# Split weight products: the low part of the weights last in each projection, and new priorities for the streams of the mixers

## The chip, the cores and the metric

The kernel runs on one core of one Trainium2 chip. The metric is the device time of one execution in microseconds (us), the median of several executions. A core has five engines with a queue each: TensorE (PE, with its weight loads shown apart as PEld), VectorE (DVE), ScalarE (ACT), GpSimd (POOL) and SyncE (SP). They wait for one another through semaphores. Matmul results land in eight banks of PSUM, and a bank is used again only when the engine that reads it out has finished.

## The reference

Two decoder layers on 256 tokens of width 1024, then a final RMSNorm. One combined projection feeds three groups of heads: gated delta net (GDN, six heads), native sparse attention (NSA, six query heads) and stick breaking (SB, four heads).

```python
for i in range(DEPTH):                      # DEPTH = 2
    hn = rmsnorm(h, ln_mix[i])
    (g_q, g_k, g_v, g_z, g_a, g_b, n_q, n_kc, n_vc, n_ks, n_vs, n_kw, n_vw, n_gate,
     s_q, s_k, s_v) = jnp.split(hn @ w_in[i], SPLIT_POINTS, axis=-1)
    o_gdn = gated_deltanet(...)
    o_nsa = native_sparse_attention(...)
    o_sb = stick_breaking_attention(s_q, s_k, s_v)
    mix = jnp.concatenate([o_gdn, head_rmsnorm(o_nsa, nsa_norm[i]), head_rmsnorm(o_sb, sb_norm[i])], axis=-1)
    h = h + mix @ w_out[i]
    h = h + conv_ffn(rmsnorm(h, ln_ffn[i]), w_up[i], ffn_conv[i], w_down[i])
    gate = jax.nn.sigmoid(rmsnorm(h, ln_ple[i]) @ w_ple_gate[i])
    h = h + gate * rmsnorm(p[i] @ w_ple[i], ple_norm[i])
return rmsnorm(h, ln_final)
```

## The kernel before

**Three products for one.** Each large matrix product is made of three. A weight piece `wr_*` comes by DMA (SP queue), ACT copies it into a rounded high part `wh_*`, and DVE subtracts the two into the low part `wl_*`, in halves of 512 columns. The activations `XH` and `XL` are split likewise. Then PE adds high times high, high times low and low times high in one bank. A piece is used for eight steps k over the width of 1024.

**The stages of a layer.** The mixers come first. PE runs their projections in the order g1, k, kcvc, g2, g3, v, q, sq, sk, sv. The pieces of k, v and q (three each) end in a causal convolution `cv` or `cq`: ACT scales the bank, and DVE adds three shifted copies, which frees the bank. Beside the projections the heads' own work runs. For NSA that is `Va`, the transposes of the rotated queries and keys to `qT` and `KH`, the split into `QQ` and `KL`, the scores (`b<-KH,QQ`, `b<-KL,QQ` and a mask), a maximum `mx` on DVE, an exponential `P` on ACT, a transpose by PE (`b<-cst,P`), a copy `PT` on ACT, and the product with `Va`. For GDN it is an inverse by a chain of some thirty small DVE operations that alternate between `prod` and `Tb`, then a copy `Tq` and matrix products with `Ta`, `Ab`, `Z` and `H`. For SB it is `L`, `b<-L,cst` and what follows. After the mixers come the output projection, the FFN (22 steps of gate `ga`, up `up` and down `dn`), and a gate.

**What sets the order.** All of it is laid out when the program is built, and each engine then runs its list as it stands. The pieces of work are generators that say what they need (`need`). `drive` looks at a model of the engines' clocks, takes those streams whose needs are met within `early` microseconds of PE's model clock, and steps the one with the lowest priority number. The projections are priority 5; `PLAN` has the numbers of the others, one dictionary for each layer. `inverse` is the chain of `Tb`, `gdn`, `nsa` and `sb` are the groups of heads, `cmp`, `compress`, `heads` and `finish` parts of NSA, `out` and `tokens` parts of GDN. `slack` and `fslack` say how far ahead of PE's model clock a weight piece may be split, in the mixers and in the rest.

`pieceA` adds one piece of k, v, q, sq, sk, and of the FFN's `ga` and `up`; `piecesB` adds those of g2, g3 and sv. `pieceA` waits per step for the low part, too:

```python
for k in range(0, KT, self.plan["step"]):
    yield self.need(0, W[1], X[1])
    self.projA(out, X, W, range(k, k + self.plan["step"]))
```

Every operation is issued through one helper, so the profile shows line L352 for nearly all; the names tell them apart.

Of the kernel before, what the change touches and what calls it, by code (L numbers as in the profile page):

```python
# [18 lines left out]
T = 256  # L19
D = 1024  # L20
KT = D // 128
HD = 64
# [400 lines left out]
class Trunk:  # L423
# [3 lines left out]
    PLAN = (dict(pace=1.0, early=0.2, slack=5, fslack=6, step=1, gdn=0, nsa=0, sb=0, inverse=2,  # L427
                 tokens=3, out=0, compress=-1, cmp=2, heads=1, finish=1, pair=4),
            dict(pace=1.1, early=0.3, slack=3, fslack=8, step=1, gdn=1, nsa=0, sb=2, inverse=2,
                 tokens=3, out=2, compress=0, cmp=4, heads=3, finish=0, pair=2))  # L430
# [221 lines left out]

    def added(self):
        return self.splitting[4] if self.splitting else self.n_split < len(self.split_seq) and self.by_transfer()

    def by_transfer(self):
        l, n, i = self.split_seq[self.n_split][:3]
        return n in self.ADDED and not self.spare(n, i) and self.n_split >= self.n_take + 2
# [277 lines left out]
    def pieceA(self, name, i, out, X, fresh=False):  # L936

        W = self.take(name, i)
        if fresh:
            mm = self.t.matmul  # L940
# [8 lines left out]
        for k in range(0, KT, self.plan["step"]):  # L949
            yield self.need(0, W[1], X[1])  # L950
            self.projA(out, X, W, range(k, k + self.plan["step"]))
        self.done()

    def piecesB(self, name, n, outs, cols, X, nk):
        for i in range(n):
            W = self.take(name, i)
            for t in range(2):
                for k in range(nk):
                    yield self.need(0, W[1], self.of(t))
                    self.projB(outs[t][:, :cols], X, W, t, i * nk, [k])  # L960
            self.done()
# [228 lines left out]
    def gdn(self, l):  # L1190
        v, a, g, gp, c, m = self.v, self.a, self.g, self.gp, self.c, self.m
        mm = self.t.matmul
# [57 lines left out]
        for r, lhs, msk, dst in ((r1, "incl", "m_strict", dec), (r2, "gt", "m_incl", decT)):  # L1250
            for x in range(2):
# [3 lines left out]
                   start=False, stop=True)  # L1255
# [24 lines left out]
        def blocks():  # L1280


            n = 24 * (64 // NB)
# [7 lines left out]
            D = self.dram.tile([2, 6, 128, 64], F32, name=f"D{l}")  # L1291
            for x in range(2):
                v.tensor_mul(fl(A[x]), bs[x][:, 0:384], fl(dec[x]))
# [13 lines left out]
            yield self.need(0, M, Tb)  # L1307
            for j in range(NB - 1):
                if j and j % 3 == 0:
                    yield self.pause(1)  # L1310
# [21 lines left out]
            yield self.need(0, F)  # L1332
            return A16, F
# [184 lines left out]
        for ch in range(4):  # L1518
            t, cp = divmod(ch, 2)
# [595 lines left out]
```

## Time and profile before

| | |
|---|---|
| median of 3 runs | 837.64 us (837.6 to 843.46) |
| the profiled execution, its own time | 837.27 us |
| its span | 835.5 us |
| mean granted TensorE clock | 0.984 |
| PE busy | 811.6 us (97%) |
| DVE busy | 626.3 us (75%) |
| ACT busy | 478.8 us (57%) |
| POOL busy | 77.4 us (9%) |
| HBM read, written | 128.29 MB, 2.03 MB |
| chain that ended last | PE 80%, DVE 10%, ACT 4%, DMA 2%, issue 2%, POOL 1% |

Busy time of matmuls is modelled at its end, so the distance from one start to the next says more than a matmul's own duration. The granted clock is 1.00 at 2.4 GHz and 0.50 at 1.2 GHz; a stretch's number is the mean over it. The first layer's mixers fill about the span's first 180 us, the second's begin near 419 us.

### The profile page before, as it was taken

How to read it: one execution, taken by the hardware profiler on the slowest of the kernel's cores; microseconds unless marked ns; L12 is line 12 of the kernel's file. 1: busy time of each engine (PE TensorE's matmuls, PEld its weight loads, DVE VectorE, ACT ScalarE, POOL GpSimd, SP SyncE). 2: the span in 40 equal slices, each digit the busy share in tenths (PEclk: the TensorE clock that was granted, in tenths of full speed). 3: DMA queues.
4: the chain of work that ended last, by engine and by line, in shares of the span. 5: the costliest groups of instructions: out<-in, count | busy, mean ns of one | idle time of the engine just before them, and what ended most of it. 6: DMA issues, size and time to landing. Idle time of an engine off the chain costs nothing.

```text
span 835.5 us, 16816 instructions
## 1 busy us (share of the span) xinstructions
PE 811.6 (97%) x6529; PEld 736.3 (88%) x6529; DVE 626.3 (75%) x1337; ACT 478.8 (57%) x1043; POOL 77.4 (9%) x151
## 2 busy tenths in 40 slices
PE   8999899999999999999999979999999999999996
PEld 6989778888999999998998868888899999999986
DVE  5748988677887788876775688967588878788755
ACT  6546474556665566554655465627476556566543
POOL 2012000211100000000301100021110000000012
PEclk9999899999999999999999997999999999999999
DMA  8645230235676677753565414203446556676501
GB/s 310 251 163 150 66 110 28 77 123 154 201 227 186 188 214 220 218 189 96 152 233 186 134 69 111 86 27 102 151 152 227 202 181 202 220 209 219 176 30 51
DMA packets 50591, 131.40 MB, mean 157 GB/s; under 512 B 17104, under 2 KB 18000, under 8 KB 50512
## 3 DMA queue, kind: packets, MB, share of 16 engines
q1 hardware_dynamic: 49056, 125.42, 47.4%
q0 software_dynamic: 1312, 4.72, 1.7%
q8 instruction: 51, 0.84, 0.4%
q14 instruction: 28, 0.23, 0.1%
q10 hardware_dynamic: 144, 0.20, 0.1%
HBM read 128.29 MB, written 2.03 MB: 156 GB/s over the span
## 4 chain that ended last, share of the span: by engine, by line
PE 80%; DVE 10%; ACT 4%; DMA 2%; issue 2%; POOL 1%; SPq 0%; POOLq 0%; DVEq 0%; ACTq 0%
PE b L352 80%; DVE wl_g L352 1%; DMA wr_w1v<-in_w_dram 1%; DVE Tb L352 1%; DVE cv L352 1%; DVE prod L352 1%; DVE oq L352 1%; ACT XH L352 1%; DMA wr_g<-in_w_dram 1%; DVE XL L352 0%; DVE QQ L352 0%; DMA wr_q<-in_w_dram 0%; ACT xh L352 0%; ACT wh_g L352 0%; DVE wl_k L352 0%
## 5 line engine op out<-in xcount | busy, mean ns | idle before, releaser
L352 DVE SCALAR_TENSOR_TENSOR u<-b,pc,u 128x255 f32<-128x255 f32 (+1 forms) x176 | 84.7, 481 | 41.1 <-ACT u L352 37.9
L352 PE MATMUL b<-XL,wh_up 128*128 128x256 f32 x352 | 99.7, 283 | 0.0
L352 PE MATMUL b<-XH,wl_up 128*128 128x256 f32 x352 | 99.6, 283 | 0.0
L352 PE MATMUL b<-XH,wh_up 128*128 128x256 f32 x352 | 99.6, 283 | 0.0
L352 PE MATMUL b<-XH,wl_ga 128*128 128x256 f32 x352 | 99.0, 283 | 0.0
L352 PE MATMUL b<-XH,wh_ga 128*128 128x256 f32 x352 | 99.0, 283 | 0.0
L352 PE MATMUL b<-XL,wh_ga 128*128 128x256 f32 x352 | 97.3, 283 | 0.0
L352 ACT ACTIVATE u<-b,pc 128x256 f32<-128x256 f32 x88 | 41.5, 472 | 74.8 <-PE b L352 74.8
L352 PE MATMUL b<-wl_dn,ah 128*128 128x512 f32 x176 | 69.3, 394 | 0.0
L352 PE MATMUL b<-wh_dn,al 128*128 128x512 f32 x176 | 69.2, 393 | 0.0
L352 PE MATMUL b<-wh_dn,ah 128*128 128x512 f32 x176 | 69.2, 393 | 0.0
L352 PEld LDWEIGHTS b<-XH,wh_ga 128*128 128x128 f32 x352 | 66.9, 190 | 1.7
L352 PEld LDWEIGHTS b<-XL,wh_ga 128*128 128x128 f32 x352 | 66.0, 190 | 1.5
L352 PEld LDWEIGHTS b<-XL,wh_up 128*128 128x128 f32 x352 | 67.1, 191 | 0.0
L352 PEld LDWEIGHTS b<-XH,wh_up 128*128 128x128 f32 x352 | 67.1, 191 | 0.0
L352 PEld LDWEIGHTS b<-XH,wl_up 128*128 128x128 f32 x352 | 67.1, 191 | 0.0
L352 PEld LDWEIGHTS b<-XH,wl_ga 128*128 128x128 f32 x352 | 67.0, 190 | 0.1
L352 DVE TENSOR_TENSOR wl_ga<-wr_ga,wh_ga 128x512 fp32r<-128x512 f32 x88 | 56.9, 688 | 6.1 <-ACT wh_ga L352 2.6
L352 DVE TENSOR_TENSOR wl_up<-wr_up,wh_up 128x512 fp32r<-128x512 f32 x88 | 56.6, 685 | 0.4
L352 DVE TENSOR_TENSOR wl_dn<-wr_dn,wh_dn 128x512 fp32r<-128x512 f32 x88 | 56.5, 684 | 0.4
L352 ACT ACTIVATE ah<-sg 128x256 fp32r<-128x256 f32 x44 | 18.4, 418 | 64.8 <-DVE sg L352 64.8
L352 ACT ACTIVATE wh_up<-wr_up 128x512 fp32r<-128x512 f32 x88 | 50.2, 620 | 0.0
(385 smaller groups left out, 2209.7 us busy)
## 6 DMA issues: line engine op xcount, KB each, us to landing
wr_ga<-in_w_dram SPq DMA_DIRECT2D x44, 512.0 KB, 3.8
wr_up<-in_w_dram SPq DMA_DIRECT2D x44, 512.0 KB, 4.2
wr_dn<-in_w_dram SPq DMA_DIRECT2D x44, 512.0 KB, 3.6
wr_out<-in_w_dram SPq DMA_DIRECT2D x16, 512.0 KB, 3.5
wr_pg<-in_w_dram SPq DMA_DIRECT2D x16, 512.0 KB, 3.3
row<-in_rows_dram POOLq DMA_DIRECT2D x8, 512.0 KB, 4.1
wr_g<-in_w_dram SPq DMA_DIRECT2D x8, 512.0 KB, 5.5
wr_g<-in_w_dram SPq DMA_DIRECT2D x8, 414.0 KB, 3.3
```

What stands on the lines that cost most here:

```text
L352: return f(*args, **kw)
```

## The change

Two things are changed. In `pieceA` and `piecesB` all products with the high part of a piece come first and wait for the high part alone; those with the low part come last and wait for it then. `pieceA` is used by the FFN as well, so the FFN's order changes too. And `PLAN` has other numbers: in the first layer seven (`early`, `slack`, `gdn`, `sb`, `inverse`, `out`, `cmp`), in the second six (`fslack`, `gdn`, `nsa`, `inverse`, `compress`, `cmp`). A flag `quiet` is added that never becomes true (`j >= 99` in a loop of fifteen) and guards a branch that the empty `ADDED` already closes. Kinds and counts of matmuls, of the operations on DVE, ACT and POOL and of the DMAs stay the same.

```diff
-    PLAN = (dict(pace=1.0, early=0.2, slack=5, fslack=6, step=1, gdn=0, nsa=0, sb=0, inverse=2,
-                 tokens=3, out=0, compress=-1, cmp=2, heads=1, finish=1, pair=4),
-            dict(pace=1.1, early=0.3, slack=3, fslack=8, step=1, gdn=1, nsa=0, sb=2, inverse=2,
-                 tokens=3, out=2, compress=0, cmp=4, heads=3, finish=0, pair=2))
+    PLAN = (dict(pace=1.0, early=0.3, slack=2, fslack=6, step=1, gdn=3, nsa=0, sb=4, inverse=4,
+                 tokens=3, out=4, compress=-1, cmp=4, heads=1, finish=1, pair=4),
+            dict(pace=1.1, early=0.3, slack=3, fslack=6, step=1, gdn=-1, nsa=3, sb=2, inverse=-2,
+                 tokens=3, out=2, compress=3, cmp=0, heads=3, finish=0, pair=2))
...
-        for k in range(0, KT, self.plan["step"]):
-            yield self.need(0, W[1], X[1])
-            self.projA(out, X, W, range(k, k + self.plan["step"]))
+        mm = self.t.matmul
+        for k in range(KT):
+            yield self.need(0, W[0], X[1])
+            for x in X:
+                mm(out, W[0][:, k], x[:, k], start=k == 0 and x is X[0], stop=False)
+        for k in range(KT):
+            yield self.need(0, W[1])
+            mm(out, W[1][:, k], X[0][:, k], start=False, stop=k == KT - 1)
         self.done()
...
-            for t in range(2):
-                for k in range(nk):
-                    yield self.need(0, W[1], self.of(t))
-                    self.projB(outs[t][:, :cols], X, W, t, i * nk, [k])
+            for q, xs in ((0, X), (1, X[:1])):
+                for t in range(2):
+                    s = slice(t * 128, t * 128 + 128)
+                    for k in range(nk):
+                        yield self.need(0, W[q], self.of(t))
+                        self.M.part = t
+                        for x in xs:
+                            mm(outs[t][:, :cols], x[:, i * nk + k, s], W[q][:, k], start=(q, i, k) == (0, 0, 0) and x is X[0],
+                               stop=(q, i, k) == (1, n - 1, nk - 1))
+                        self.M.part = None
```

The first place is DVE in the mixers of the second layer, where the chain of `Tb` and `prod` ends. Before, the row of the maxima `mx` of the first two heads stands directly behind the chain:

```order
L352 TENSOR_TENSOR prod<-Mb,Tb 96x15
L352 TENSOR_TENSOR Tb<-Tb,prod 96x15
L352 CAST Tq<-Tb 96x256 x2
L352 TENSOR_REDUCE mx<-b 128x2 x4
L352 SCALAR_TENSOR_TENSOR cv<-b,pc_193,cv 128x255
L352 SCALAR_TENSOR_TENSOR cv<-b,pc_193,cv 128x254
L352 SCALAR_TENSOR_TENSOR cv<-b,pc_193,cv 128x253
L352 TENSOR_TENSOR wl_q<-wr_q,wh_q 128x512 x2
```

And now the same end of the chain:

```order
L352 TENSOR_TENSOR prod<-Mb,Tb 96x15
L352 TENSOR_TENSOR Tb<-Tb,prod 96x15
L352 CAST Tq<-Tb 96x256 x2
L352 SCALAR_TENSOR_TENSOR cv<-b,pc_193,cv 128x255
L352 SCALAR_TENSOR_TENSOR cv<-b,pc_193,cv 128x254
L352 SCALAR_TENSOR_TENSOR cv<-b,pc_193,cv 128x253
L352 TENSOR_TENSOR KL<-b,KH_6095 64x512
L352 TENSOR_TENSOR QQ_6093<-qT,QQ_6093 64x768
L352 TENSOR_TENSOR KL<-b,KH_6096 64x512
L352 TENSOR_TENSOR QQ_6094<-qT,QQ_6094 64x768
```

The chain moved ahead of the splits `KL` and `QQ`: 17 of its operations stand ahead of the last two rotations of the keys (`kr` and `ropet`), and 12 behind them. The maxima come two `cv` and four `wl_q` rows after `QQ`, clear of the chain.

The second place is ACT there, from `Va` on. Before, the copy of the first q piece stands behind `Va`:

```order
L352 ACTIVATE Va<-b 128x4x64 x2
L352 ACTIVATE wh_q<-wr_q 128x512 x2
L352 ACTIVATE qT<-b 128x3x128 x2
L352 ACTIVATE KH_6030<-b 64x512
L352 ACTIVATE KH_6031<-b 64x512
L352 ACTIVATE KH_6030<-KH_6030 64x512
L352 ACTIVATE QQ_6028<-qT 64x768
L352 ACTIVATE KH_6031<-KH_6031 64x512
L352 ACTIVATE QQ_6029<-qT 64x768
L352 ACTIVATE cv<-b,pc_193 128x256 x3
```

And now:

```order
L352 ACTIVATE Va<-b 128x4x64 x2
L352 ACTIVATE cv<-b,pc_193 128x256
L352 ACTIVATE qT<-b 128x3x128 x2
L352 ACTIVATE KH_6095<-b 64x512
L352 ACTIVATE KH_6096<-b 64x512
L352 ACTIVATE KH_6095<-KH_6095 64x512
L352 ACTIVATE QQ_6093<-qT 64x768
L352 ACTIVATE KH_6096<-KH_6096 64x512
L352 ACTIVATE QQ_6094<-qT 64x768
L352 ACTIVATE cv<-b,pc_193 128x256
L352 ACTIVATE wh_q<-wr_q 128x512 x2
```

The copy `wh_q` of the first q piece moved behind the whole preparation of `KH` and `QQ` and behind two `cv`. On PE the first twelve products of that piece now stand ahead of the first scores; before, the scores of the first two head pairs stood among the products of v, ahead of all of q.

The third place is DVE in the first layer, where the chain begins. Before, the splits stand ahead of the chain, and two `cv` as well:

```order
L352 TENSOR_TENSOR QQ_975<-qT,QQ_975 64x768
L352 SCALAR_TENSOR_TENSOR cv<-b,pc_189,cv 128x255
L352 SCALAR_TENSOR_TENSOR cv<-b,pc_189,cv 128x254
L352 SCALAR_TENSOR_TENSOR cv<-b,pc_189,cv 128x253
L352 TENSOR_TENSOR wl_q<-wr_q,wh_q 128x512 x2
L352 SCALAR_TENSOR_TENSOR cv<-b,pc_189,cv 128x255
L352 SCALAR_TENSOR_TENSOR cv<-b,pc_189,cv 128x254
L352 SCALAR_TENSOR_TENSOR cv<-b,pc_189,cv 128x253
L352 TENSOR_TENSOR Tb<-Tb,Mb 96x15
L352 TENSOR_TENSOR prod<-Mb,Tb 96x28
```

And now, from the fifth operation of the chain on:

```order
L352 TENSOR_TENSOR Tb<-Tb,prod 96x13x3
L352 TENSOR_TENSOR KL<-b,KH_981 64x512
L352 TENSOR_TENSOR QQ_979<-qT,QQ_979 64x768
L352 TENSOR_TENSOR KL<-b,KH_982 64x512
L352 TENSOR_TENSOR QQ_980<-qT,QQ_980 64x768
L352 TENSOR_TENSOR prod<-Mb,Tb 96x48
L352 TENSOR_TENSOR Tb<-Tb,prod 96x12x4
```

Five operations of the chain moved ahead of the splits, twelve more stand between `QQ` and the first `cv` of v, and the last twelve and `Tq` between the first `cv` and the second; the `mx` of the first heads come behind the second `cv`.

## Rows read from the trace of the kernel before

**Rows 1.** The page: busy time, share and count of each engine.
```profile
PE 811.6 (97%) x6529; PEld 736.3 (88%) x6529; DVE 626.3 (75%) x1337; ACT 478.8 (57%) x1043; POOL 77.4 (9%) x151
```

**Rows 2.** Busy time by stretches of 20 us, with the granted clock (PEclk).
```profile
core 0: us, PE busy (x) PEld busy (x) DVE busy (x) ACT busy (x) POOL busy (x), PEclk, DMA share, GB/s
...
80.00:100.00 20.00, 16.77 (x124) 14.39 (x122) 18.52 (x63) 10.45 (x27) 0.45 (x1) 0.95 0.16 47
100.00:120.00 20.00, 18.95 (x166) 15.82 (x165) 18.30 (x47) 13.92 (x28) 2.44 (x5) 0.88 0.49 136
...
220.00:240.00 20.00, 20.00 (x142) 18.74 (x141) 17.92 (x35) 13.02 (x29) 0.92 (x2) 1.00 0.72 217
...
480.00:500.00 20.00, 14.95 (x118) 13.88 (x116) 15.97 (x50) 11.92 (x28) 0.66 (x2) 0.94 0.21 79
500.00:520.00 20.00, 19.95 (x154) 16.57 (x153) 17.00 (x44) 9.60 (x24) 1.38 (x3) 0.72 0.42 112
...
560.00:580.00 20.00, 18.83 (x158) 16.66 (x159) 13.91 (x34) 13.45 (x28) 6.31 (x7) 1.00 0.29 94
```

**Rows 3.** Timeline of PE in the first layer's FFN: start, duration, operation, idle before.
```profile
250.07 0.28 PE L352 MATMUL b<-XH,wh_ga 128*128 128x256 f32 x1
...
250.90 0.28 PE L352 MATMUL b<-XL,wh_ga 128*128 128x256 f32 x1
```

**Rows 4.** Groups of PE's instructions: busy, mean ns, idle before and releasers.
```profile
L352 PE MATMUL b<-cst,P 128*128 128x128 f32 x72 | 11.8, 304 | 5.5 <-DVE mx L352 4.6 <-ACT P L352 0.9
...
L352 PE MATMUL b<-KH,QQ 128*128 128x256 f32 (+1 forms) x24 | 8.7, 427 | 3.8 <-DVE cq L352 1.7 <-DVE on L352 1.0 <-DVE QQ L352 0.9
L352 PE MATMUL b<-L,cst 128*128 128x384 f32 (+1 forms) x32 | 7.9, 388 | 0.9 <-DVE L L352 0.9
```

**Rows 5.** Timeline of PE in the second layer, scores, q, and transposes of P.
```profile
486.98 0.28 PE L352 MATMUL b<-KH,QQ 128*128 128x256 f32 x1
...
491.19 0.28 PE L352 MATMUL b<-XH,wh_q 128*128 128x256 f32 x1
...
493.95 0.28 PE L352 MATMUL b<-XH,wl_q 128*128 128x256 f32 x1
498.84 1.54 PE L352 MATMUL b<-cst,P 128*128 128x128 f32 x6 [4.61 <-DVE mx L352]
```

**Rows 6.** Timeline of DVE there: last rotation, chain's first, maxima.
```profile
479.76 0.35 DVE L352 TENSOR_TENSOR ropet<-b,sin 128x64 f32<-128x64 f32 x2
...
489.01 0.18 DVE L352 TENSOR_TENSOR Tb<-Tb,Mb 96x15 f32<-96x15 f32 x1
...
497.72 1.41 DVE L352 TENSOR_REDUCE mx<-b 128x2 f32<-128x256 f32 x4
```

**Rows 7.** Timeline of ACT there, from Va to the convolutions.
```profile
479.75 0.85 ACT L352 ACTIVATE Va<-b 128x256 f32<-128x256 f32 x2 [1.36 <-DVE ropet L352]
480.49 1.14 ACT L352 ACTIVATE wh_q<-wr_q 128x512 fp32r<-128x512 f32 x2
481.53 0.86 ACT L352 ACTIVATE qT<-b 128x384 f32<-128x384 f32 x2
...
486.39 0.84 ACT L352 ACTIVATE cv<-b,pc 128x256 f32<-128x256 f32 x2
```

**Rows 8.** Timeline of DVE in the first layer: split, chain, convolutions.
```profile
80.08 0.95 DVE L352 TENSOR_TENSOR QQ<-qT,QQ 64x768 fp32r<-64x768 f32 x1
...
88.05 0.20 DVE L352 TENSOR_TENSOR prod<-Mb,Tb 96x48 f32<-96x48 f32 x1
...
90.94 1.50 DVE L352 SCALAR_TENSOR_TENSOR cv<-b,pc,cv 128x255 f32<-128x255 f32 x3
...
95.14 0.58 DVE L352 CAST Tq<-Tb 96x256 f16<-96x256 f32 x2
95.63 1.51 DVE L352 SCALAR_TENSOR_TENSOR cq<-b,pc,cq 128x255 f32<-128x255 f32 x3
```

**Rows 9.** Timeline of PE in the first layer, the first product of q.
```profile
84.68 0.28 PE L352 MATMUL b<-XH,wh_q 128*128 128x256 f32 x1
```

More of the change, by code (lines that the diff above doesn't have):

```diff
@@ L651 @@
     ADDED = ()
+    quiet = False
     def added(self):
@@ L657, in by_transfer @@
         l, n, i = self.split_seq[self.n_split][:3]
-        return n in self.ADDED and not self.spare(n, i) and self.n_split >= self.n_take + 2
+        return n in self.ADDED and not self.spare(n, i) and not self.quiet and self.n_split >= self.n_take + 2
     def split_to(self, n):
@@ L948, in pieceA @@
             return
-        for k in range(0, KT, self.plan["step"]):
-            yield self.need(0, W[1], X[1])
-            self.projA(out, X, W, range(k, k + self.plan["step"]))
+        mm = self.t.matmul
[6 more added lines that the diff above has]
+            mm(out, W[1][:, k], X[0][:, k], start=False, stop=k == KT - 1)
         self.done()
     def piecesB(self, name, n, outs, cols, X, nk):
+        mm = self.t.matmul
         for i in range(n):
             W = self.take(name, i)
-            for t in range(2):
-                for k in range(nk):
-                    yield self.need(0, W[1], self.of(t))
-                    self.projB(outs[t][:, :cols], X, W, t, i * nk, [k])
+            for q, xs in ((0, X), (1, X[:1])):
[8 more added lines that the diff above has]
+                        self.M.part = None
             self.done()
@@ L1291, in blocks @@
             D = self.dram.tile([2, 6, 128, 64], F32, name=f"D{l}")
+            self.quiet = False
             for x in range(2):
@@ L1307, in blocks @@
             yield self.need(0, M, Tb)
+            self.quiet = False
             for j in range(NB - 1):
+                self.quiet = j >= 99
                 if j and j % 3 == 0:
@@ L1332, in blocks @@
             yield self.need(0, F)
+            self.quiet = False
             return A16, F
```

## Prediction

> **What bounds the kernel now.** I read the busy time of the engines first. PE is busy for 97% of the span, and the next engine for 75% [rows 1]. So only time in which PE stands, or runs at its lower clock, can be won; the change removes no matmul. Next the stretches of 20 us show where such time lies. In the FFN PE is busy for 20.00 of 20 us at a granted clock of 1.00 (220 to 240 us) [rows 2]. The mixers have three bad places: 80 to 120 us in the first layer (16.77 and 18.95 us busy, clock 0.95 and 0.88), 480 to 520 us in the second (14.95 us busy and then a clock of 0.72), and 560 to 580 us (18.83 us busy) [rows 2]. The groups of PE's instructions then name what PE waited for: DVE's `mx` for 4.6 us ahead of the transposes of `P`, and DVE's `cq`, `on` and `QQ` for 1.7, 1.0 and 0.9 us ahead of scores [rows 4]. The timelines of PE, DVE and ACT give the order of events. So in the mixers DVE, busy with the chain of `Tb`, is what ends last.
>
> **What the low clock costs.** The clock has two levels, 2.4 and 1.2 GHz, so a mean of 0.88 is a low level in 24% of the stretch. In the first layer the low time is 20 x (0.10 + 0.24) = 6.8 us, in the second 20 x (0.12 + 0.56) = 13.6 us, from the clocks of [rows 2]. Work done then takes twice as long, so at most 3.4 and 6.8 us are lost. The part of the low time in which PE stands anyway costs nothing: if all of the low time before 100 us and before 500 us (2.0 and 2.4 us) lay in waits, the loss would be 2.4 and 5.6 us. I take 3.1 and 6.1, together 9.2 us, with 8.0 and 10.2 as the ends. The clock fell after the 4.6 us wait for `mx`, and in the first layer after waits of 1.7 and 1.0 us close together [rows 2, 4]. The Trainium skill, "TensorE: Matmul & The Clock Gate", section Terms, puts the penalty at the throttled time times the withheld share of the clock, which would be 10.2 us for these stretches and an end about 1 us lower than mine. That page counts low time in waits as well; the trace here has such time, so I stay with 9.2.
>
> **The products' order by itself: nothing in the FFN.** Matmuls with 256 columns start 0.12 us apart whichever product follows which (eight starts from 250.07 to 250.90, seven steps of 0.119 us) [rows 3]. High products first and low products last are the same 24 starts, and where PE never waits (20.00 of 20 us) a later need for the low part saves nothing. What hides a late low part there is PE's own backlog; if it were gone, a whole DVE subtraction would show. I cost the FFN at 0, with 0 to 1 us as the bound, since a stretch without idle time could only lose. In the mixers the order matters only with the new priorities.
>
> **First layer, 80 to 110 us.** Before, PE waited 1.7 (`cq`), 1.0 (`on`), half of 0.9 (`QQ`, shared by both layers) and 0.9 us (ACT `P`): 4.05 us [rows 4]. Now twelve operations of the chain stand between the last `QQ` and the first `cv` of v. The split `QQ` ends at 81.03; twelve such operations took 90.94 - 88.05 = 2.9 us, and three rows of `cv` 1.5 us, so the bank of the first `cv` is free at 81.03 + 2.9 + 1.5 = 85.4 [rows 8]. That is the bank that q's first piece takes, and PE comes to it at 84.68 [rows 9]: a wait of 0.7 us. The next twelve operations are the shorter ones (95.14 - 90.94 - 1.5 = 2.7 us), `Tq` takes 0.5 and the second `cv` 1.5 [rows 8], so q's second piece gets its bank at 90.1. PE has 24 products of 0.12 us to do and arrives at 85.4 + 2.9 = 88.3: a wait of 1.8 us. With some 0.35 us for `P` the new waits come to 2.85, and 4.05 - 2.85 = 1.2 us are won. From below, the second wait is nothing if DVE gets there in time (3.0 us won); from above, the waits are as long as before (nothing won). The five chain operations put ahead of `KL` fit into DVE's idle time there.
>
> **Second layer, 480 to 515 us.** Before: 4.6 us for `mx` and half of 0.9 for `QQ`, 5.05 us [rows 4]. The chain ran from 489.01 to 497.2, and `mx` came only at 497.72, while PE had done its last product of q and stood from 493.95 to 498.84 [rows 5, 6]. With the chain ahead of the splits this wait goes. What is late next is the first q piece. Seventeen chain operations (17 x 0.24 = 4.1 us, from [rows 8]) come ahead of the rotation that ended at 480.11 [rows 6], so `Va`, which waits for that, moves from 479.75 to 483.85 [rows 7]. ACT then runs `Va` (0.74), one `cv` (0.4), and from `qT` to the second `cv` 486.39 - 481.53 = 4.86 us as before; another 0.4 for that `cv`, and half of `wh_q`'s 1.04 us, make the first half of `wh_q` ready at 490.8 [rows 7]. PE arrives earlier than before: q's first product started at 491.19 behind scores that took 491.19 - 486.98 less 15 products of v (1.8 us), so 2.4 us, which now come later; that gives 488.8 [rows 5]. New wait: 2.0 us. Behind it on ACT stand the next `cv` and the other q pieces, for which PE may wait another 1.0 us (0 to 1.8). Won: 5.05 - 3.0 = 2.05 us, with 0.5 and 5 as ends.
>
> **The rest.** The lower `slack` and later GDN work in the first layer leave less split in advance; around the compression and g2 I put 0.7 us of new waits (0 to 1.5, the larger being near the 1.7 us wait for `cq` [rows 4]). The wait for `L` ahead of `b<-L,cst`, 0.9 us in the second layer [rows 4], goes, since 42 products of sv now stand in between; in the first layer SB, now at priority 4, has less work beside it, and I charge the same 0.9 there. Together 0.
>
> **Sum.** From the profiled execution's 837.27: -1.2 - 2.05 + 0.7 = -2.55 us of waits, and -9.2 us of low clock if the clock no longer falls: 825.5. The median of the runs shown (837.64) is 0.4 above that execution, so about 826. In general the time is 826 us plus half of the time that PE runs low.
>
> **The rivals.** *One clock fall stays.* Two waits near 2 us are left, one in each layer. For a fall speaks the first layer before, where waits of 1.7 and 1.0 us with work between went ahead of one; against it, that these were two in a row, and that the new ones stand by themselves. A fall as long as that one (6.8 us low) gives 826 + 3.4 = 829.4. *The holes only move.* Both new waits bring the clock down as before (6.8 and 13.6 us low, less the waiting): 826 + 3.4 + 6.1 = about 835.5, no change by measure. A page has a rule that speaks for this: the Trainium skill, "TensorE: Matmul & The Clock Gate", section What's actually happening, calls the throttled state the default, which activity releases. By that rule any wait may bring the clock down, and the kernel would gain the 2.5 us of waits only; the trace bears it out in part, since the clock is at 1.00 in 560 to 580 us with 1.2 us of PE idle [rows 2]. *The change does nothing.* If the bound were PE's sum of work, the end would stay at 837; the 3.23 and 5.05 us idle in 80 to 100 and 480 to 500 us speak against it [rows 2]. *Slower.* The clock stays low through the second layer's q and sq: the copy `wh_q` of the first piece stands on ACT behind eight operations that hang on the chain (place: `Va` to `wh_q`), so each later q and sq piece can be late in turn and PE keeps stopping. The six pieces are 6 x 24 x 0.12 = 17 us of PE work, 35 us at the lower clock: 826 + 17.5 + some 5 us of waits = 848. It decides once the low time passes 40 us (826 + 20 = 846); before it was 20.4 us.
>
> **How the numbers follow.** About 1% is what a measurement of this kernel can tell from no change, so faster ends at 829.3 and slower begins at 846.0. Chances: no fall, 826, 0.45, and 0.05 that the waits come out still smaller, near 820; one fall, 829.4, 0.25, of which about a third lies below the bound; holes move, 835.5, 0.12; nothing, 837, 0.06; slower, 848, 0.07. That is 0.58 for faster, 0.35 for same, 0.07 for slower. The range goes down to 819, where the new waits of 2.85 and 3.0 us are nearly all absent, and up to 838, which leaves out the slower case and little more. For the likeliest case alone it is 822 to 829.
>
> **What would show it.** Right: no wait of `b<-cst,P` for `mx` in the second layer; a wait ahead of the first `wh_q` product there of about 2 us, ended by ACT; in the first layer waits ahead of q's first and second pieces of 0.7 and 1.8 us, ended by DVE's `cv`; a granted clock of 1.00 in all stretches from 80 to 120 and 480 to 520 us; FFN stretches unchanged at 20.00 us. Wrong: a clock below 0.9 in any of these stretches, a wait above 3 us for `wh_q`, or a loss in the FFN.

## The result and the profile after

| | before | changed |
|---|---|---|
| median, timed side by side | 840.37 us (837.6 to 843.46) | 830.06 us (828.29 to 831.35) |
| ratio, 95% interval | | 0.9879 (0.9833 to 0.9924) |
| profiled execution, its own time | 837.27 us | 831.35 us |
| its span | 835.5 us | 829.6 us |
| its mean granted clock | 0.984 | 0.993 |

The kernel is 1.2% faster. Ratios, here and below, are those on record with their 95% intervals, and need not be the quotient of the medians beside them. Of the four executions before, two were at 837.6 us and two above 843; in the 102 that came later its median was 838.0 us, and against that one the changed kernel is 7.9 us faster, not 10.3. The predicted time was 826 us, 4 us under the measured median and inside the range of 819 to 838. Between the two profiled executions 5.9 us went: the second layer begins 1.9 us earlier, and the rest was won in its mixers. The number of matmuls is the same (6529), and PE's busy time fell from 811.6 [rows 1] to 804.4 us; PE's idle time did not fall, it went from 835.5 - 811.6 = 23.9 us to 829.6 - 804.4 = 25.2 us.

The page and the stretches of the changed kernel, which answer to [rows 1] and [rows 2]. The columns are those of [rows 2]: busy time of PE, PEld, DVE, ACT and POOL, the granted clock, the DMA share and GB/s.

```profile
PE 804.4 (97%) x6529; PEld 730.5 (88%) x6529; DVE 627.5 (76%) x1339; ACT 477.7 (58%) x1041; POOL 76.7 (9%) x151
```

```profile
0.00:20.00 20.00, 16.79 (x82) 11.77 (x83) 9.78 (x29) 13.68 (x37) 4.48 (x20) 1.00 0.81 290
...
80.00:100.00 20.00, 17.09 (x131) 14.89 (x130) 18.59 (x59) 8.90 (x23) 0.46 (x1) 1.00 0.24 57
100.00:120.00 20.00, 19.29 (x255) 16.82 (x254) 19.07 (x50) 17.85 (x39) 2.55 (x6) 1.00 0.40 120
...
220.00:240.00 20.00, 20.00 (x136) 18.48 (x135) 18.05 (x36) 13.82 (x30) 0.60 (x1) 1.00 0.76 222
...
480.00:500.00 20.00, 18.22 (x155) 16.91 (x154) 19.07 (x56) 14.14 (x33) 0.92 (x2) 1.00 0.34 92
500.00:520.00 20.00, 17.71 (x198) 14.15 (x198) 18.54 (x44) 15.21 (x32) 1.95 (x4) 0.83 0.44 147
...
560.00:580.00 20.00, 19.78 (x141) 17.19 (x140) 13.94 (x32) 15.18 (x32) 4.95 (x6) 1.00 0.35 106
```

The two bad stretches of the first layer are at a clock of 1.00 now (0.95 and 0.88 before). In the second layer the clock fell once more in this execution, to a mean of 0.83 in 500 to 520 us, where it was 0.72; 20 x 0.17 x 2 = 6.8 us low, in place of 13.6 in 480 to 520 us. One more stretch was low before, and the prediction passed over it:

```profile
0.00:20.00 20.00, 17.41 (x78) 12.72 (x79) 10.72 (x31) 13.96 (x37) 4.48 (x20) 0.91 0.85 305
```

These 3.6 us low at the start are gone in the changed kernel's profile, but that is not the change's doing for sure: among the runs below, some profiles with the new numbers have them (after_fill, 0.91) and some do not. PE's busy time in 80 to 100 us has hardly grown (16.77 us then, 17.09 now): the waits there were traded for others, and the clock was won.

What PE waits for now, which answers to [rows 4]: engine and line, what it waited for, us in total, times, the longest.

```profile
PE b L352 <- ACT wh_q L352: 3.4, 2, 1.8
PE b L352 <- ACT XH L352: 1.7, 5, 0.6
PE b L352 <- ACT wh_g L352: 1.5, 1, 1.5
PE b L352 <- ACT PT L352: 1.3, 2, 1.0
...
PE b L352 <- DVE oq L352: 1.0, 1, 1.0
...
PE b L352 <- DVE prod L352: 0.8, 1, 0.8
PE b L352 <- ACT P L352: 0.8, 1, 0.8
```

The waits for `mx`, `cq`, `on` and `L` of [rows 4] are gone. In their place stand, by the profile's names, `wh_q` (once in each layer), `wh_g`, `PT`, `oq` and `prod`. In time order, from the timeline of PE:

```profile
38.88 0.50 PE L352 MATMUL b<-wh_g,XH 128*128 128x512 f32 x1 [1.46 <-ACT wh_g L352]
...
86.59 0.36 PE L352 MATMUL b<-XH,wh_q 128*128 128x256 f32 x1 [0.78 <-DVE prod L352]
...
91.28 0.36 PE L352 MATMUL b<-XH,wh_q 128*128 128x256 f32 x1 [1.59 <-ACT wh_q L352]
...
488.73 0.39 PE L352 MATMUL b<-XH,wh_q 128*128 128x256 f32 x1 [1.78 <-ACT wh_q L352]
...
507.90 0.37 PE L352 MATMUL b<-Z,Ta 64*64 64x64 f16 x12 [0.77 <-ACT P L352]
508.42 0.35 PE L352 MATMUL b<-Ta,id 64*64 64x384 f16 x2
508.58 0.38 PE L352 MATMUL b<-Ta,Z 64*64 64x64 f16 x12
508.88 0.66 PE L352 MATMUL b<-cst,P 128*128 128x128 f32 x4
510.54 1.70 PE L352 MATMUL b<-Va,PT 128*128 128x65 f32 x8 [1.00 <-ACT PT L352]
```

The waits of 0.7, 1.8 and 2.0 us that the prediction worked out for q are there with 0.78, 1.59 and 1.78 us. In the first layer the profile names `prod` and `wh_q` as what ended them, but the rows of DVE and ACT speak for the bank of a `cv`, as predicted:

```profile
84.93 1.52 DVE L352 SCALAR_TENSOR_TENSOR cv<-b,pc,cv 128x255 f32<-128x255 f32 x3
...
89.63 1.50 DVE L352 SCALAR_TENSOR_TENSOR cv<-b,pc,cv 128x255 f32<-128x255 f32 x3
```

```profile
86.22 1.14 ACT L352 ACTIVATE wh_q<-wr_q 128x512 fp32r<-128x512 f32 x2
89.73 0.47 ACT L352 ACTIVATE cq<-b,pc 128x256 f32<-128x256 f32 x1 [2.37 <-PE b L352]
90.10 1.14 ACT L352 ACTIVATE wh_q<-wr_q 128x512 fp32r<-128x512 f32 x2
```

The two rows of `cv` end at 86.45 and 91.13 us, and PE starts 0.14 and 0.15 us later. The layer has six copies `wh_q`, two for a piece; the second pair ended at 87.36, so that the pair at 90.10 is the third piece's, for which the second need not wait.

The stretch of low clock comes behind the last rows: matmuls of 64 by 64 with two waits of about 1 us among them, a place that the prediction did not name. Its own sign of being wrong, a clock below 0.9 in 500 to 520 us, is there.

**Executions of one program differ, and by the clock.** In the jobs of the experiments the kernel before was run 102 times. Its instructions are the same each time, its times are not: 834.3 to 834.9 us where the mean granted clock was 0.992 (15 executions), 835.7 to 839.0 at 0.983 to 0.987 (44), 841.8 to 844.0 at 0.977 to 0.982 (41), 845.3 and 845.7 at 0.976. From 0.992 to 0.978 the low time grows by 0.014 x 835 x 2 = 23 us, and the time by 8.8 us: 0.38 us for each low microsecond, under the prediction's half; some of the low time falls in waits. The Trainium skill, "TensorE: Matmul & The Clock Gate", section Terms, counts the full half; the executions here show less. The changed kernel's four executions are two at 828.3 and 828.9 us (clock 0.995 and 0.996) and two at 831.3 us (0.991 and 0.993).

### The profile page after: what moved, and what is told of

The parts are those of the page before. It is cut to its first block, busy times and chain, and to the rows that moved or that the text cites. A ratio compares the mean times of both kernels' runs of the same rounds, so it can differ in the third digit from the quotient of the medians.

```text
span 829.6 us, 16807 instructions
## 1 busy us (share of the span) xinstructions
PE 804.4 (97%) x6529; PEld 730.5 (88%) x6529; DVE 627.5 (76%) x1339; ACT 477.7 (58%) x1041; POOL 76.7 (9%) x151
## 4 chain that ended last, share of the span: by engine, by line
PE 79%; DVE 10%; ACT 6%; DMA 2%; issue 1%; POOL 1%; SPq 0%; POOLq 0%; DVEq 0%; ACTq 0%
PE b L352 79%; DMA wr_g<-in_w_dram 1%; ACT XH L352 1%; DVE wl_g L352 1%; DVE wl_v L352 1%; DVE ck L352 1%; ACT L L352 1%; DVE XL L352 1%; ACT wh_g L352 1%; ACT KH L352 0%; ACT xh L352 0%; DMA wr_w1v<-in_w_dram 0%; ACT P L352 0%; DVE prod L352 0%; DVE Tb L352 0%
## 5 line engine op out<-in xcount | busy, mean ns | idle before, releaser
L352 PE MATMUL b<-XH,wh_up 128*128 128x256 f32 x352 | 86.4, 283 | 0.0
L352 PE MATMUL b<-XL,wh_up 128*128 128x256 f32 x352 | 86.4, 283 | 0.0
L352 PE MATMUL b<-XH,wh_ga 128*128 128x256 f32 x352 | 86.2, 282 | 0.0
L352 PE MATMUL b<-XL,wh_ga 128*128 128x256 f32 x352 | 84.6, 283 | 0.0
L352 PE MATMUL b<-XH,wl_ga 128*128 128x256 f32 x352 | 51.1, 283 | 0.0
L352 ACT ACTIVATE wh_dn<-wr_dn 128x512 fp32r<-128x512 f32 x88 | 50.2, 621 | 0.0
L352 ACT ACTIVATE wh_ga<-wr_ga 128x512 fp32r<-128x512 f32 x88 | 50.1, 617 | 0.0
L352 PE MATMUL b<-XH,wl_up 128*128 128x256 f32 x352 | 49.4, 283 | 0.0
```

The costliest lines, as they stand in the source:

```text
L352: return f(*args, **kw)
```

## The experiments

Times are medians, each with its ratio to the kernel before in the same job. That kernel's median was 838.02 us beside the first four rows, 841.78 beside slack5, ffn_old, l1slack4 and before_filled, 837.69 beside slack3, two_numbers and before_fill_q, and 837.83 beside after_fill. Medians of different jobs differ by up to 4 us for this alone.

| kernel | us, lowest to highest | ratio to before, interval |
|---|---|---|
| order_only | 848.81 (840.62 to 850.34) | 1.0095 (1.0055 to 1.0136) |
| plan_only | 839.23 (838.64 to 840.51) | 0.9991 (0.9960 to 1.0021) |
| plan_first | 835.24 (831.76 to 840.99) | 0.9945 (0.9908 to 0.9982) |
| plan_second | 840.66 (836.85 to 842.18) | 1.0019 (0.9991 to 1.0047) |
| slack5 | 840.82 (838.32 to 846.28) | 1.0006 (0.9970 to 1.0042) |
| slack3 | 836.86 (834.73 to 840.91) | 0.9985 (0.9951 to 1.0020) |
| two_numbers | 832.77 (829.97 to 835.09) | 0.9912 (0.9881 to 0.9944) |
| ffn_old | 829.90 (828.43 to 837.67) | 0.9893 (0.9854 to 0.9932) |
| l1slack4 | 833.68 (831.47 to 840.19) | 0.9933 (0.9897 to 0.9970) |
| before_filled | 839.17 (837.01 to 847.34) | 1.0018 (0.9978 to 1.0058) |
| before_fill_q | 839.46 (833.08 to 840.17) | 0.9984 (0.9951 to 1.0017) |
| after_fill | 832.77 (828.47 to 835.76) | 0.9921 (0.9891 to 0.9951) |

### The order alone, and the plan alone

order_only is the changed kernel with the old plan in both layers, so the order of the products is all that differs from before:

```diff
-    PLAN = (dict(pace=1.0, early=0.3, slack=2, fslack=6, step=1, gdn=3, nsa=0, sb=4, inverse=4,
-                 tokens=3, out=4, compress=-1, cmp=4, heads=1, finish=1, pair=4),
-            dict(pace=1.1, early=0.3, slack=3, fslack=6, step=1, gdn=-1, nsa=3, sb=2, inverse=-2,
-                 tokens=3, out=2, compress=3, cmp=0, heads=3, finish=0, pair=2))
+    PLAN = (dict(pace=1.0, early=0.2, slack=5, fslack=6, step=1, gdn=0, nsa=0, sb=0, inverse=2,
+                 tokens=3, out=0, compress=-1, cmp=2, heads=1, finish=1, pair=4),
+            dict(pace=1.1, early=0.3, slack=3, fslack=8, step=1, gdn=1, nsa=0, sb=2, inverse=2,
+                 tokens=3, out=2, compress=0, cmp=4, heads=3, finish=0, pair=2))
```

> The changed kernel with the old numbers of the plan in both layers: only the order of the products is changed (low part last). Theory (the numbers of the plan move the chain of Tb, and that is what takes the holes away): in the second layer the maxima of the first heads still stand behind the whole chain on VectorE, so a wait of 3 to 5 us for mx and a stretch of low clock stay there, and the first layer keeps waits near 4 us and its low clock: 835 to 841 us, within 0.5% of the kernel before. Rival (the order brings most of the gain, since TensorE can start a piece once its high part is there): 828 to 833 us.

It is slower than before by 0.95%, and by 10.8 us in the medians, worse than either theory allowed. At like clocks (0.978, 0.982, 0.987) its executions are 4 to 5 us above those of the kernel before; the rest goes with its lower clock. Its stretches:

```profile
100.00:120.00 20.00, 17.64 (x118) 15.09 (x117) 19.01 (x52) 14.58 (x29) 2.80 (x5) 0.74 0.56 159
180.00:200.00 20.00, 16.63 (x65) 12.92 (x64) 10.15 (x21) 6.71 (x12) 3.42 (x4) 0.83 0.42 126
...
460.00:480.00 20.00, 19.94 (x126) 16.86 (x127) 6.24 (x14) 4.39 (x11) 0.00 (x0) 0.66 0.34 122
500.00:520.00 20.00, 15.77 (x105) 14.61 (x105) 18.44 (x56) 8.93 (x22) 0.00 (x0) 0.83 0.22 45
```

And two rows of its timeline of PE:

```profile
187.38 0.88 PE L352 MATMUL b<-cst,zs 128*128 128x128 f32 x3 [2.70 <-DVE zs L352]
...
511.82 0.56 PE L352 MATMUL b<-XH,wh_q 128*128 128x256 f32 x1 [3.70 <-DVE cv L352]
```

The projections run ahead. The first product of sq starts at 107.5 us (114.0 before), that of sk at 132.3 (142.3). A piece that asks for its high part alone is ready sooner, so the projections are laid out sooner, and less of them is left to lie beside the end of GDN: PE waits 2.7 us for `zs`, GDN's last product, ahead of the output projection, with the clock down (180 to 200 us, 0.83). In the second layer the second piece of q waits 3.7 us for the bank of a `cv` that stands behind the chain. And in 460 to 480 us the clock is 0.66 while PE is busy for 19.94 of 20 us: the profile shows no wait ahead of the fall. What PE does there is the compression, runs of matmuls of only 45 columns:

```profile
461.46 2.85 PE L352 MATMUL b<-X,wr_w1k 128*128 128x45 f32 x20
464.10 0.77 PE L352 MATMUL b<-wh_g,XH 128*128 128x512 f32 x1
464.68 0.63 PE L352 MATMUL b<-wh_g,XL 128*128 128x512 f32 x1
465.10 0.92 PE L352 MATMUL b<-X,wr_w1k 128*128 128x45 f32 x4
465.81 0.77 PE L352 MATMUL b<-wh_g,XH 128*128 128x512 f32 x1
466.38 0.63 PE L352 MATMUL b<-wh_g,XL 128*128 128x512 f32 x1
466.81 5.18 PE L352 MATMUL b<-X,wr_w1v 128*128 128x45 f32 x24
```

plan_only is the reverse, the kernel before with all thirteen new numbers; its products keep this form:

```diff
+        for k in range(0, KT, self.plan["step"]):
+            yield self.need(0, W[1], X[1])
+            self.projA(out, X, W, range(k, k + self.plan["step"]))
```

> The kernel before with the new numbers of the plan in both layers: products as before (high, high, low in each step). Theory (the plan takes the holes away, the order helps only at the start of a piece): the wait for mx is gone, but the first piece of q in the second layer now waits for its low part, too, which VectorE subtracts behind KL and QQ: 1 to 2 us more of waiting than in the changed kernel there, some in the first layer; 829 to 836 us. Rival (the order is the main thing): 836 to 841 us, like before.

No gain either. Its mean clock is high (0.990 to 0.993 in all ten executions), but PE stands for longer (28.9 us in place of 23.9 in the profiled executions). The longest wait is for the low part:

```profile
89.93 0.39 PE L352 MATMUL b<-XH,wl_q 128*128 128x256 f32 x1 [3.29 <-DVE wl_q L352]
```

With the chain put earlier the subtraction `wl_q` comes later, and a piece that needs both halves in its first step stands for it. In the changed kernel the same piece does its 16 products with the high part first. plan_only also waits 3.2 us for `QQ` and 2.4 us for `L`; no run takes these apart. At 0.992 two executions are at 839.1 and 839.5 us, 4.6 us and more above the kernel before at that clock: what the better clock gives, the waits take. So the two halves of the change need each other: the theory that the plan does it alone (829 to 836 us) is wrong, and so is the rival for order_only, that the order does it.

### One layer's plan at a time

plan_first is the changed kernel with the old numbers back in the second layer, plan_second with the old numbers back in the first:

```diff
-            dict(pace=1.1, early=0.3, slack=3, fslack=6, step=1, gdn=-1, nsa=3, sb=2, inverse=-2,
-                 tokens=3, out=2, compress=3, cmp=0, heads=3, finish=0, pair=2))
+            dict(pace=1.1, early=0.3, slack=3, fslack=8, step=1, gdn=1, nsa=0, sb=2, inverse=2,
+                 tokens=3, out=2, compress=0, cmp=4, heads=3, finish=0, pair=2))
...
-    PLAN = (dict(pace=1.0, early=0.3, slack=2, fslack=6, step=1, gdn=3, nsa=0, sb=4, inverse=4,
-                 tokens=3, out=4, compress=-1, cmp=4, heads=1, finish=1, pair=4),
+    PLAN = (dict(pace=1.0, early=0.2, slack=5, fslack=6, step=1, gdn=0, nsa=0, sb=0, inverse=2,
+                 tokens=3, out=0, compress=-1, cmp=2, heads=1, finish=1, pair=4),
```

> The changed kernel with the new numbers of the first layer only; the second layer has the old ones. Theory: the first layer ends as in the changed kernel (no low clock between 80 and 120 us, 2 us earlier than before at the start of the second layer), the second keeps the wait behind the chain for mx and its low clock: 833 to 838 us. Rival (the order alone mends the second layer): 828 to 832 us, as the changed kernel.

> The changed kernel with the new numbers of the second layer only; the first layer has the old ones. Theory: the first layer keeps its waits of 1 to 2 us for cq and on or the like and about 6.8 us of low clock, the second is as in the changed kernel: 830 to 835 us. If parts add up, the gain of this one and that of the first layer alone, both counted from the kernel with the order alone, make the whole difference between that one and the changed kernel. Rival (the holes only move between the layers, or the order alone gives the gain): within 1 us of the kernel with the order alone.

plan_first came in its theory's range, though its second layer waits 3.1 us for the bank of a `cv` and not for `mx`; plan_second came 5.7 us above its theory's range, and not within 1 us of order_only as its rival had it. Counted from the order alone (848.81), the first layer's numbers give 13.6 us, the second's 8.2, and both together (830.06, from another job) 18.8, 3.0 less than the sum of the two.

### Which numbers

slack5 is the changed kernel with 5 for slack in the first layer, slack3 the same with 3:

```diff
-    PLAN = (dict(pace=1.0, early=0.3, slack=2, fslack=6, step=1, gdn=3, nsa=0, sb=4, inverse=4,
+    PLAN = (dict(pace=1.0, early=0.3, slack=5, fslack=6, step=1, gdn=3, nsa=0, sb=4, inverse=4,
```

> The changed kernel with slack back at 5 in the first layer, all else new. Theory (the lower slack delays the split of the weights, and so causes the wait of 1.5 us for wh_g near 38 us that the kernel before did not have): that wait is gone. But the pieces split earlier take VectorE's time ahead of the chain of Tb, so that Q and K splits, maxima and convolutions come later: the holes of the first layer between 85 and 110 us come back, with low clock; 831 to 838 us. Rival (the slack only costs that wait): 827 to 829 us.

> The changed kernel with slack 3 in place of 2 in the first layer, all else new. With 5 there the first layer loses 10 us (projections run ahead, and the end of GDN stands alone). Theory (how far the projections run ahead of the heads' work is what this number sets, by degrees): between the two, q to sq earlier than in the changed kernel by 2 to 4 us and a wait for zs of 1 to 3 us near 185 us: 832 to 838 us. Rival (a threshold between 2 and 3 or 3 and 5; the wait of 1.5 us for wh_g near 38 us goes and nothing comes for it): 826 to 830 us.

One number of the thirteen undoes the whole gain (840.82 us, and 838 at most was expected). With slack 5 the wait for `wh_g` near 38 us is gone as expected, sq starts at 108.8 us, and `zs` is late again:

```profile
PE b L352 <- DVE zs L352: 4.3, 2, 4.1
PE b L352 <- ACT P L352: 2.5, 2, 1.7
```

With slack 3 there is no wait for `zs`, and sq starts at 118.3 us, later than in the changed kernel (114.6), against the theory that it goes by degrees; the time alone fell in its range. The loss there is another: a wait of 3.1 us at 93.26 us for the bank of a `cv` behind the chain, and low clock. The program's chain then stands behind `KL` and `QQ` as it did before. So slack does two things in the first layer: between 5 and 3 it keeps the projections back, and between 3 and 2 it lets the chain's first five operations go ahead of the splits.

two_numbers has the new order of the products and the old plan but for slack in the first layer and compress in the second:

```diff
-    PLAN = (dict(pace=1.0, early=0.2, slack=5, fslack=6, step=1, gdn=0, nsa=0, sb=0, inverse=2,
+    PLAN = (dict(pace=1.0, early=0.2, slack=2, fslack=6, step=1, gdn=0, nsa=0, sb=0, inverse=2,
...
-                 tokens=3, out=2, compress=0, cmp=4, heads=3, finish=0, pair=2))
+                 tokens=3, out=2, compress=3, cmp=4, heads=3, finish=0, pair=2))
```

> The changed kernel with two of the thirteen new numbers only: slack 2 in the first layer and compress 3 in the second; the other eleven are the old ones. In the program these two put the chain of Tb where the changed kernel has it (in the first layer five operations ahead of KL and QQ, in the second 11 in place of 17 ahead of the last rotations, and all of it ahead of KL and QQ). Theory (the chain's place and the pace of the projections are the whole gain, the other numbers are by the way): 828 to 833 us. Rival (the priorities of gdn, sb, out and inverse are needed to keep work for the tails): waits of 2 us and more for zs or oq near 160 to 190 us with low clock, 834 to 841 us.

These two give 832.77 us, most of the way, as its theory had it. By the medians the other eleven are worth 2.7 us, but the intervals of the two ratios overlap, so that this is not shown. That `compress` moves the chain in the second layer, and `inverse` and `gdn`, whose names say so, do not, is seen in two traces. two_numbers and plan_first differ there in `compress` alone (3 and 0), with `inverse` at 2 and `gdn` at 1 in both: the chain begins at 475.66 us, ahead of `KL` and `QQ`, in the first, and at 485.12 us, behind them, in the second.

### The FFN

ffn_old is the changed kernel with this at the head of `pieceA`:

```diff
+        if name in ("ga", "up"):
+            for k in range(KT):
+                yield self.need(0, W[1], X[1])
+                self.projA(out, X, W, range(k, k + 1))
+            self.done()
+            return
```

> The changed kernel with the FFN's gate and up pieces in the old order (high, high, low in each step). Theory (the order is worth nothing where TensorE never waits): both FFNs keep 189 us from their first gate product to the first product of the gate behind them, and the time stays within 1 us of the changed kernel: 829 to 831 us. Rival (products with the low part last let VectorE fall behind without a wait, and the FFN gained from it): 832 us or more, with waits for wl_ga or wl_up.

829.90 us against 830.06: nothing, as predicted. Its stretch of the FFN is at 20.00 us and 1.00, too:

```profile
220.00:240.00 20.00, 20.00 (x140) 18.66 (x139) 18.24 (x36) 13.23 (x30) 0.00 (x0) 1.00 0.72 231
```

### The wait for wh_q

l1slack4 is the changed kernel with 4 for slack in the second layer:

```diff
-            dict(pace=1.1, early=0.3, slack=3, fslack=6, step=1, gdn=-1, nsa=3, sb=2, inverse=-2,
+            dict(pace=1.1, early=0.3, slack=4, fslack=6, step=1, gdn=-1, nsa=3, sb=2, inverse=-2,
```

> The changed kernel with slack 4 in place of 3 in the second layer. The copy wh_q of the first q piece then stands ahead of the preparation of KH and QQ on ScalarE. Theory (that place is what makes TensorE wait 1.8 us for wh_q): the wait ahead of the first q product in the second layer is gone or under 0.5 us, and the time is 1 to 2 us less than that of the changed kernel: 826 to 830 us, if nothing else comes late for it. Rival (another wait takes its place: the rotations of the keys stand behind the whole chain now): waits of 1.5 us or more for the transposes of kr or for QQ, and 830 to 835 us.

The rival was right in the time and in that other waits take the place, though not for the things that it named. The wait ahead of q's first product is gone, and near it three others came: `Va`, `wh_v`, and `wh_q` of the next piece.

```profile
483.88 0.84 PE L352 MATMUL b<-cst,kr 128*128 128x128 f32 x4 [0.59 <-ACT Va L352]
485.22 0.39 PE L352 MATMUL b<-XH,wh_v 128*128 128x256 f32 x1 [0.50 <-ACT wh_v L352]
492.88 0.39 PE L352 MATMUL b<-XH,wh_q 128*128 128x256 f32 x1 [1.65 <-ACT wh_q L352]
```

Their sum is 2.7 us, 1.0 more than what it removed (`r` and `Y` add 0.9 and 0.6 elsewhere); with more low clock (0.74 in 500 to 520 us) it is 833.68 us.

### The clock by itself

To part a wait from the clock behind it, the wait of 4.6 us in the kernel before was to be filled with idle matmuls (their result is thrown away) and nothing else moved. before_filled puts these lines into the heads' generator, ahead of the transposes of P:

```diff
+                if l == 1 and (t, r) == (0, 0):
+                    for _ in range(19):
+                        self.t.e.matmul(bs[0], self.identb, m["m_causal"][:, None, :].to_broadcast([128, 4, 128]), start=True, stop=True)
```

> The kernel before, with nineteen idle matmuls (512 columns, the identity times a mask, overwritten by the transposes that follow) put into the second layer's wait of 4.8 us ahead of the first transposes of P. Every other instruction stands where it stood; the wait is filled, not shortened. Theory (most of what the wait cost was the low clock behind it): the granted clock in 500 to 520 us goes from 0.72 to 0.95 or more, and the time falls by 5 to 7 us, to 830 to 833 us. Rival (the waits themselves are the cost, or the clock falls for the small matmuls of the stage anyway): clock below 0.85 there and 836 to 839 us; if the fillers end after P is ready, slower by what they overhang, up to 1 us.

This one says nothing on either theory: the bank `bs[0]` is one that the scores held, so the first idle matmul itself waited 4.6 us for `mx`, and the wait was not filled. before_fill_q takes the bank that q's next piece holds already, which nobody reads once the second `cv` is done:

```diff
+                if l == 1 and (t, r) == (0, 0):
+                    for _ in range(18):
+                        self.t.e.matmul(self.tiles[6], self.identb, m["m_causal"][:, None, :].to_broadcast([128, 4, 128]), start=True, stop=True)
```

> The kernel before, with eighteen idle matmuls (512 columns each, overwritten by the q products that follow) in the bank that q's second piece holds already, so that they need not wait for P; they lie in the second layer's wait of 4.8 us ahead of the first transposes of P. All else stands where it stood. The bank is free once the second cv of v is done (494.5 us), so they fill some 4 us from there, and the wait for mx goes down to 0.5 to 1 us while nothing gets done sooner. Theory (most of what this wait costs is the low clock behind it): the granted clock in the stretch behind the wait is 0.95 or more instead of 0.72, and the time is 4 to 7 us less than before: 831 to 834 us. Rival (the wait itself costs it, or the clock falls for the small matmuls of this stage anyway): clock below 0.85 there and 836 to 840 us.

```profile
480.00:500.00 20.00, 19.56 (x148) 18.84 (x147) 15.69 (x41) 11.86 (x23) 1.75 (x3) 1.00 0.40 135
500.00:520.00 20.00, 19.08 (x133) 13.57 (x131) 19.11 (x57) 11.36 (x29) 0.92 (x2) 1.00 0.34 89
```

```profile
501.08 4.06 PE L1674 MATMUL b<-mb,identb 128*128 128x512 bf16 x18 [0.35 <-DVE cv L352]
```

With the wait filled the clock stays at 1.00 behind it in the profiled execution. From the first q product to the first sq product it takes 526.95 - 497.69 = 29.3 us, where it was 524.72 - 491.19 = 33.5: 4.2 us, although nothing was ready sooner. So of this hole of 4.6 us the wait itself could not be had back by filling, and the low clock behind it cost 4.2 us more. The median of the whole did not fall (839.46 us), against the theory, so that a gain of the whole by filling is not shown. Three executions, with a mean clock of 0.992 to 0.994, were at 833.1 to 833.9 us; the other seven, at 0.985 and 0.986, at 838.6 to 840.2. The profiled one is of the seven. There the clock fell in the first layer's compression, whose instructions are those of the kernel before, and was 0.83 in 60 to 80 and 100 to 120 us, too:

```profile
40.00:60.00 20.00, 19.14 (x98) 16.39 (x98) 8.17 (x22) 9.43 (x23) 3.35 (x8) 0.83 0.48 170
```

after_fill does the same on the changed kernel, in the wait for `PT` ahead of its fall near 511 us, in the bank of the products with `Va`:

```diff
+                if l == 1 and (t, r) == (0, 2):
+                    for _ in range(5):
+                        self.t.e.matmul(obs, self.identb, m["m_causal"][:, None, :].to_broadcast([128, 4, 128]), start=True, stop=True)
```

> The changed kernel with five idle matmuls (512 columns each) in the bank that the products of Va and PT then overwrite, in the second of the two waits of about 1 us that stand ahead of the fall of the clock near 511 us in the second layer (the wait for PT at 509.5 us). Nothing gets done sooner. Theory (the clock falls there for the waits of 1.0 and 1.2 us among matmuls of 64 by 64): nearly all executions come out without that fall, at 828 to 829 us with a mean clock of 0.995 or more, a median 1 to 3 us under that of the changed kernel. Rival (one wait filled is not enough, or the small matmuls alone bring the clock down): a mean clock of 0.991 to 0.993 in half of the executions or more, and a median of 830 to 832 us.

In the profiled execution the clock held through 500 to 520 us (1.00), but it fell elsewhere: from 494 us on, behind the wait of 1.79 us for `wh_q`, in the first layer's compression (0.76 in 40 to 60 us), and at the start (0.91 in 0 to 20 us). The median is 832.77 us, above what theory and rival allowed and no better than the changed kernel, so filling this one wait does not pay. Whether it prevents the fall at that place in general stays open; one profile shows it.

## Why the prediction was right, and where it was not

**What bounds the kernel.** Right: only waits and low clock changed, nearly all of it in the mixers. The FFN takes the same time, and undoing its new order changes nothing (ffn_old).

**The waits.** Right for the three places that it worked out: the waits for `mx` (4.6), `cq`, `on` and `L` went, and 0.7, 1.8 and 2.0 us ahead of q came as 0.78, 1.59 and 1.78, each within a quarter of a microsecond. That the first two hang on the bank of a `cv` fits the rows, though the profile names other releasers. The sum of the waits was wrong. It said 2.55 us less; in the profiled executions PE stands for 25.2 us in place of 23.9, 1.3 us more, just beyond the end of the prediction's own bounds (0 and 0.5 won, 1.5 lost: 1.0 more).

**The rest: a term that was mis-sized.** It was put at 0.7 us for lower slack and at 0 for SB. One wait of 1.46 us for `wh_g` took the place of the first, at the upper end of its bounds; no wait for `L` is left in either layer, but 0.99 us for `oq` came. With smaller waits, 0.62 us for `XH` at the start the largest, the waits outside the prediction's two stretches grew by about 3 us. In the second layer 0.77 and 1.00 us came among matmuls of 64 by 64, where the sum had 1.0 us, for q.

**The low clock: the other term that was mis-sized.** The sum took back all 9.2 us. The step that failed is the one that tied a fall to the two waits near 2 us. Neither brought one in the profiled execution; the fall came 20 us behind the second, after the waits of 0.77 and 1.00 us. It depends on the execution: in the profile of ffn_old, whose mixers have the changed kernel's order, the clock did fall right behind the wait of 1.76 us for `wh_q` (0.91 in 480 to 500 us), and again in 500 to 520 us (0.83). Two of the four executions have a mean clock lower by about as much as that fall makes (0.991 and 0.993 against 0.995 and 0.996), and they take 831.3 - 828.6 = 2.7 us longer; that it is the same fall in the one that was not profiled is not shown. The rival of one fall (829.4, a chance of 0.25) was thus as true as the forecast, and the measured median of 830.06 lies by it. The price of a low microsecond was right: a half at most, 0.38 measured over the 102 executions.

**How much was wait and how much clock** stays open. In the two profiled executions all of the gain is PE's busy time: 811.6 - 804.4 = 7.2 us less for the same matmuls, and 1.3 us more of standing. At like mean clocks the changed kernel is ahead by about 3.2 us (834.3 to 834.9 us before at 0.992, 831.3 at 0.991 and 0.993, two executions), which leaves 7 us of the 10.3 for the clock, or 4.7 of the 7.9 against the median of 102. The two need not clash: a PE at the low level gives the other engines time, so that some waits may have been hidden before (0.05 us idle in 500 to 520 us at 0.72, 2.29 us at 0.83 now). No run keeps the clock up through a whole execution of the kernel before, and that would part them.

**What was luck.** The errors add up. Against the profiled execution's 831.35 us the sum of 825.5 was 5.9 us too low, 3.9 of it from the waits and 2.0 from the clock; the forecast stands nearer to the median only since two of the four executions did better. The range of 819 to 838 us held even the case of no change (837), so that its holding says little.

**The parts of the change.** The prediction laid the gain to the plan and costed the order at nothing with it, and lower slack as a loss. The runs showed otherwise: the order alone costs 10.8 us, as the projections run ahead of the work that they should cover, and the lower slack, a price in the sum, is what holds them back; with slack 5 all of the gain is gone. The total did not suffer from this, since it was summed from the changed kernel's built order, in which both are in.

**The other rivals.** By PE's idle time the holes did only move; what kept that rival's 835.5 us away is that the moved ones brought the clock down less. Nor was the kernel slower. But the kind of case that the slower rival feared is real, and order_only is it: behind the first 20 us, five stretches of low clock and a median of 849 us, in part over holes that one half of the change opens when the other half is missing.

## What to carry to other kernels

Where products can be put in any order, let those come first whose operands are ready first; but a stream that becomes ready sooner also runs sooner, so look at what it was covering at the end of the stage, and hold it back there. A hole on PE can cost twice, by itself and by the clock behind it, so a plan is judged by the falls of the clock that it leaves as well as by the sum of its waits; plan_only has few falls and yet gains nothing. When the executions of one program fall into groups, read their granted clocks before comparing medians: groups of like clock set the falls aside, as far as a mean can.

## What was not expected of the hardware

The clock came down where the profile shows no wait of PE. In order_only it was 0.66 in 460 to 480 us, with PE busy for 19.94 of 20 us; plan_second, which has the new numbers there, shows it more clearly still:

```profile
460.00:480.00 20.00, 20.00 (x143) 15.92 (x143) 7.54 (x16) 5.72 (x14) 0.00 (x0) 0.83 0.46 132
```

```profile
460.45 2.92 PE L352 MATMUL b<-X,wr_w1k 128*128 128x45 f32 x20
```

In both the clock fell within a run of 20 matmuls of 45 columns, and the longest wait in the 9 us ahead of it was 0.15 us or less. before_fill_q fell at such a run too (0.83 in 40 to 60 us), but 10 us after waits of 0.23, 0.22 and 0.44 us. Such runs alone do not do it: the kernel before has them in 40 to 60 us at a clock of 1.00. The Trainium skill, "TensorE: Matmul & The Clock Gate", section What's actually happening, says that activity releases a throttle which is the default; the stretches of order_only and plan_second agree with that reading, and not with one in which only a wait brings the clock down. And a wait filled with matmuls whose result is thrown away kept the clock up, in the one execution that was profiled, and made the work behind it 4.2 us shorter.
